# Where the mixer's weight splits are made: three pairs split in the feed-forward, fewer splits on GpSimd, and a rotation that does not wait for its scale

## The chip, the core and the metric

One core of one Trainium2 chip runs the kernel. The metric is device time in microseconds (us), the median of several runs: 1210.14 us before the change (three runs, 1209.3 to 1210.4). The engines are TensorE (PE in the profile, its weight loads PEld), VectorE (DVE), ScalarE (ACT), GpSimd (POOL) and SyncE (SP), which issues the weight loads from HBM.

## The reference

Two layers of an encoder on x of 256 positions by 1024 channels, all in float32:

```python
for l in range(DEPTH):
    x = x + 0.5 * swiglu(rms_norm(x, ffn1_norm[l]), ffn1_w_gate[l], ffn1_w_up[l], ffn1_w_down[l])
    h = rms_norm(x, mix_norm[l])
    u = h @ w_in[l]
    z, xbc, dt_raw, q_lat, kv_lat, k_pe, c_h, c_b, c_c = jnp.split(u, pts, axis=-1)
    ...
    x = x + jnp.concatenate([y_ssd, y_mla, y_conv], axis=-1) @ w_out[l]
    x = x + 0.5 * swiglu(rms_norm(x, ffn2_norm[l]), ffn2_w_gate[l], ffn2_w_up[l], ffn2_w_down[l])
```

The mixer has three branches: a state-space branch (SSD) in both directions over chunks of 128 positions, latent attention (MLA) with 8 heads of 96 channels, 32 of them rotated by position, and a gated convolution. In the attention, q and k are made by two small products from normalised latents, each head's q and k is divided by its root mean square, the last 32 channels are rotated, and softmax attention follows.

## The kernel before, in words

A float32 weight is used as the sum of two numbers that TensorE multiplies in one pass each. For this every weight unit (128 x 1024, or a little less) is loaded into a `raw` tile by SyncE (`issue_dma`, L292), rounded by ScalarE into `whi` (L309), and the rest is subtracted into `wlo` by VectorE or GpSimd (L311, both in `issue_split`). A product is then three matmuls: high by high, high by low, low by high (`mm3`, L435 to L437, or the same three in `project`, `down` and `tokens_mm`). Activations are split likewise after a transposition through PSUM (`split_scaled`, L430 and L432). `whi` and `wlo` have six slots each (`WB`), `raw` three.

The list `specs` holds the loads in the order of use, two units to a load as a rule. `next_unit` hands out the next unit and, before that, issues the splits of the units up to two uses ahead (`AHEAD_SPLIT`). Which splits go to GpSimd stands in `POOL_FFN` (6 of a feed-forward's units, by their place in it) and `POOL_MIX` (24 of a mixer's 55). TensorE's order is the order of the program, written out by hand. The order on the other engines is set by a planner that runs the program on a model of the times; `behind` adds an order where the kernel wants one.

A feed-forward runs over six groups of its 2816 columns (five of 512, one of 256): gate, up, then the down products of the group before. A mixer has a list `main` of units that TensorE works off: after the time-step and latent columns (`tq`) and a first z unit, pairs of 256 columns of `w_in` named in `ORDER`: `('x', i)` are two units of SSD channels (`xbc_unit`), `('c', i)` two of the convolution (`conv_unit`), `('z', i)` one of the gate in two halves, and `('u', 0)` the projection of q, k and v from the latents (`mla_project`). Then come 16 units of `w_out`. `SIDE` says before which place of `main` other work stands on TensorE: the latents' transposes before place 4 (`latents`, L859), the B-C products before 9 (`cb_products`, L870), the transposes of q before 12 and of k before 13 (`mla_transpose`, L957), then per head the scores, the transposes of the probabilities (`mla_turn`, L983) and the products with v, from place 14.

In a channel unit VectorE adds up the convolution's taps (L812) and forms the SiLU (L817). In the convolution branch it does L1032 to L1040, with the transposes at L703. In the attention, `mla_project` copies q and k, sums squares per head (L919), takes the reciprocal root on VectorE (`rsqrt`, L346 to L360), and then calls `mla_rope` for each half of the positions: k is multiplied by its scale (L938, VectorE), and q's and k's last 32 channels are rotated by 12 GpSimd instructions (L943 to L946). In `mla_scores`, VectorE takes the negative maximum of a head's scores for both halves (L972) and multiplies it by q's scale (L974, two numbers per partition); ScalarE's exponential (L977) takes scale and maximum from there. In the SSD heads VectorE does L1113 and L1114.

The buffers `yk` (four of 8 KB a partition) and `b4` (six of 4 KB) belong to the mixer: `yk` holds the transposed q and k and the branches' outputs (and in the first feed-forward the parameter rows), `b4` holds the gate, q and k, and the SSD's tokens and sums.

Of the kernel before, what the change touches and what calls it, by code (L numbers as in the profile page):

```python
# [34 lines left out]
BF16 = mybir.dt.bfloat16  # L35
AHEAD_DMA, AHEAD_SPLIT = 2, 2
WB, NT2, NT1 = 6, 15, 13
# [3 lines left out]

ORDER = [('x', 4), ('c', 0), ('u', 0), ('x', 5), ('x', 1), ('c', 1), ('x', 3), ('x', 0), ('x', 2), ('c', 2), ('c', 3), ('c', 4), ('z', 3), ('c', 5), ('z', 1), ('z', 2)]
SIDE = {'latents': 4, 'cb': 9, 'decays': 6, 'f3': 17, 'qT': 12, 'kT': 13, 'xs0': 18, 'xs1': 22, 'mla': 14, 'mla_b': 1, 'mla_c': 2, 'st': 26, 'mla_out': 23, 'mla_end': 29, 'conv_out': 28, 'conv_end': 30, 'ssd': 18, 'ssd_b': 4, 'end0': 31, 'turn0': 36, 'end1': 40, 'turn1': 42}
POOL_FFN, POOL_MIX = [0, 1, 2, 3, 4, 6], [2, 3, 11, 12, 14, 16, 17, 20, 21, 22, 23, 25, 26, 27, 32, 34, 36, 38, 39, 40, 41, 42, 45, 49]
FREE_FFN, FREE_MIX = [], [4, 5]
# [10 lines left out]
def trunk(ctx: ExitStack, tc: tile.TileContext, I: dict, out: bass.AP):  # L56
# [154 lines left out]

    specs = []

    def cols(w, l, c0, n):
        return w[l, :, c0:c0 + n].rearrange("(k p) f -> p k f", p=P)

    def add(ap, shape, units):
        specs.append((ap, shape, units))

    two = [(slice(None), slice(0, P)), (slice(None), slice(P, 256))]  # L220
# [6 lines left out]

    def spec_ffn(l, n):
        wg, wu, wd = I[f"{n}_w_gate"], I[f"{n}_w_up"], I[f"{n}_w_down"]

        def gu(f0, n):
            for w in (wg, wu):
                if n == 512:
                    for q in range(2):
                        add(w[l, q * 512:(q + 1) * 512, f0:f0 + n].rearrange("(k p) f -> p k f", p=P), (4, n), rr2)
                else:
                    add(cols(w, l, f0, n), (KT, n), kk)

        for i, (f0, n) in enumerate(GROUPS):
            gu(f0, n)  # L240
            if i > 0:
                p0, pn = GROUPS[i - 1]
                for f in range(p0, p0 + pn, 256):
                    rows2(wd[l, f:f + 256, :])
        for f in range(f0, f0 + n, 256):
            rows2(wd[l, f:f + 256, :])

    def spec_mix(l):
# [5 lines left out]
        for kind, i in ORDER:  # L254
            if kind == "x":
                add(cols(w, l, OFF_XBC + i * 256, 256), (KT, 256), two)
            elif kind == "c":
                add(cols(w, l, (OFF_CC, OFF_CH, OFF_CB)[i % 3] + i // 3 * 256, 256), (KT, 256), two)
            elif kind == "z":
                add(cols(w, l, OFF_Z + i * 256, 256), (KT, 256), kk)  # L260
            else:
                add(I["mla_w_uq"][l].rearrange("(k p) f -> p k f", p=P), (2, 768), rr)
                add(I["mla_w_ukv"][l].rearrange("(k p) f -> p k f", p=P), (1, 1024),
                    [(slice(0, 1), slice(None))])
        for c in (6, 7, 4, 5, 0, 1, 2, 3):
            rows2(I["w_out"][l, c * 256:(c + 1) * 256, :])

    pool_units, free_units = set(), set()
    for l in range(DEPTH):
        for n in ("ffn1", "mix", "ffn2"):  # L270
            first = sum(len(s[2]) for s in specs)
            if n == "mix":
# [5 lines left out]
            if first:  # L278
                pool_units.update(first + i for i in (POOL_MIX if n == "mix" else POOL_FFN))
                free_units.update(first + i for i in (FREE_MIX if n == "mix" else FREE_FFN))  # L280

# [17 lines left out]
    def issue_split(i):  # L299
# [6 lines left out]
        _, a, b = src.shape  # L306
        hi = whi.tile([P, 1024], F32R, tag="whi", name=nm("whi"))[:, :a * b].rearrange("p (a b) -> p a b", b=b)
        lo = wlo.tile([P, 1024], F32R, tag="wlo", name=nm("wlo"))[:, :a * b].rearrange("p (a b) -> p a b", b=b)
        i_hi = A.activation(out=hi, in_=src, func=AF.Copy)  # L309
# [20 lines left out]
    def prefetch(n):  # L330
        while st["unit"] <= min(st["use"] + n, len(flat)) - 1:
            issue_split(st["unit"])
            st["unit"] += 1

    def next_unit():
        prefetch(1 + AHEAD_SPLIT)
        i = st["use"]
        st["use"] += 1
        return units.pop(i)

# [378 lines left out]
    def mixer(l, norm, nxt):  # L719
# [168 lines left out]
        def mla_project():  # L888
# [3 lines left out]
            for t in range(NT):  # L892
# [69 lines left out]
        def mla_scores(hh):  # L962
# [191 lines left out]
        for kind, i in ORDER:  # L1154
# [113 lines left out]
```

## Time and profile before

| | us |
|---|---|
| median of 3 runs | 1210.14 |
| lowest, highest | 1209.3, 1210.4 |
| the profiled execution | 1209.31 |
| its span, first to last instruction | 1207.6 |
| TensorE's mean granted clock in it | 0.997 |
| TensorE matmuls busy | 1175.3 |
| VectorE busy | 779.0 |
| ScalarE busy | 656.9 |
| GpSimd busy | 265.7 |

The span is cut into stages here: first feed-forward of layer 0 up to about 200 us, mixer to 415, second feed-forward to 612, then layer 1 with its feed-forward to 797, mixer to 1012 and feed-forward to the end. A table by stretches gives busy time and, in brackets, the number of instructions of each engine, then the granted clock of TensorE, the DMA engines' busy share and the rate. A line of a wait view reads: who waited, for whom, total us, how often, the longest. An instruction that stands still after it has begun counts as busy.

### The profile page before, as it was taken

To read this page: it belongs to the slowest core of one execution; us is meant where nothing else is said; L and a number is where in the kernel's file an instruction comes from. 1 tells how busy PE (TensorE), PEld (TensorE's weight loads), DVE (VectorE), ACT (ScalarE), POOL (GpSimd) and SP (SyncE) were. 2 spreads that over 40 slices of the span, in tenths; PEclk is the share of its full clock that TensorE was granted. 3 is DMA by queue.
4 is the path that set the end of the run, shared out by engine and by line. 5 is a ranking of instruction groups with operands and counts; after the bars stand their busy time and mean duration, and the time that the engine had idled before them with its cause. 6 is when DMAs were issued, how large, how long until landed. Compare 5 with 4: busy or idle time off the path is not lost.

```text
span 1207.6 us, 17054 instructions
## 1 busy us (share of the span) xinstructions
PE 1175.3 (97%) x6540; PEld 1012.8 (84%) x6540; DVE 779.0 (65%) x1283; ACT 656.9 (54%) x1120; POOL 265.7 (22%) x303
## 2 busy tenths in 40 slices
PE   9999999989999999999999999999899999999998
PEld 6888888979978888888888888889799788888887
DVE  6554576898698665554465455469987976555553
ACT  7444456757656564444474444376577556544441
POOL 1140011785252310000040000027832513000000
PEclk9999999999999999999999999999999999999999
DMA  8665554434323465555465555535343334655550
GB/s 281 219 206 176 196 177 132 157 105 133 117 102 140 140 209 180 203 179 201 144 209 188 195 176 196 177 114 165 116 140 106 105 140 151 219 187 175 195 187 35
DMA packets 105537, 198.51 MB, mean 164 GB/s; under 512 B 4014, under 2 KB 47314, under 8 KB 105456
## 3 DMA queue, kind: packets, MB, share of 16 engines
q1 hardware_dynamic: 104288, 197.14, 48.5%
q8 instruction: 51, 0.84, 0.3%
q0 software_dynamic: 1152, 0.28, 0.2%
q14 instruction: 30, 0.25, 0.1%
q10 hardware_dynamic: 16, 0.00, 0.0%
HBM read 196.36 MB, written 1.05 MB: 163 GB/s over the span
## 4 chain that ended last, share of the span: by engine, by line
PE 80%; DVE 11%; ACT 3%; POOL 3%; issue 2%; DMA 0%; SPq 0%; ACTq 0%; DVEq 0%; POOLq 0%
PE ps L577 13%; PE ps L576 13%; PE ps L580 13%; PE ps L528 7%; PE ps L529 7%; PE ps L532 7%; PE ps L437 4%; PE ps L435 4%; PE ps L436 4%; PE ps L599 2%; PE ps L663 1%; DVE wlo L311 1%; PE ps L660 1%; PE ps L661 1%; DVE t L812 1%
## 5 line engine op out<-in xcount | busy, mean ns | idle before, releaser
L309 ACT ACTIVATE whi<-raw 128x1024 fp32r<-128x1024 f32 (+2 forms) x374 | 391.8, 1057 | 394.6 <-PE ps L580 229.7
L311 DVE TENSOR_TENSOR wlo<-raw,whi 128x1024 fp32r<-128x1024 f32 (+1 forms) x308 | 386.5, 1258 | 304.3 <-ACT whi L309 303.6
L576 PE MATMUL ps<-whi,h 128*128 128x512 f32 (+1 forms) x768 | 284.1, 374 | 0.0
L577 PE MATMUL ps<-wlo,h 128*128 128x512 f32 (+1 forms) x768 | 283.4, 373 | 0.1
L311 POOL TENSOR_TENSOR wlo<-raw,whi 128x1024 fp32r<-128x1024 f32 (+2 forms) x66 | 159.4, 2424 | 560.3 <-ACT whi L309 529.0
L580 PE MATMUL ps<-whi,h 128*128 128x512 f32 (+1 forms) x768 | 223.4, 372 | 0.0
L577 PEld LDWEIGHTS ps<-wlo,h 128*128 128x128 f32 x768 | 145.1, 189 | 25.4 <-DVE wlo L311 0.4
L576 PEld LDWEIGHTS ps<-whi,h 128*128 128x128 f32 x768 | 145.0, 189 | 25.1
L580 PEld LDWEIGHTS ps<-whi,h 128*128 128x128 f32 x768 | 140.5, 189 | 25.2
L437 PE MATMUL ps<-h,wlo 128*128 128x256 f32 x384 | 109.4, 285 | 4.5 <-DVE wlo L311 3.1
L435 PE MATMUL ps<-h,whi 128*128 128x256 f32 x384 | 110.8, 288 | 0.1
L436 PE MATMUL ps<-h,whi 128*128 128x256 f32 x384 | 108.8, 283 | 0.0
L528 PE MATMUL ps<-whi,t2r 128*128 128x512 f32 x256 | 101.1, 395 | 0.0
L529 PE MATMUL ps<-wlo,t2r 128*128 128x512 f32 x256 | 99.7, 389 | 0.0
L532 PE MATMUL ps<-whi,t2r 128*128 128x512 f32 x256 | 78.9, 389 | 0.0
L437 PEld LDWEIGHTS ps<-h,wlo 128*128 128x128 f32 x384 | 73.7, 192 | 5.3 <-DVE wlo L311 3.5
L435 PEld LDWEIGHTS ps<-h,whi 128*128 128x128 f32 x384 | 73.9, 192 | 1.2 <-ACT xs L883 0.6
L436 PEld LDWEIGHTS ps<-h,whi 128*128 128x128 f32 x384 | 73.9, 192 | 0.1
L532 PEld LDWEIGHTS ps<-whi,t2r 128*128 128x128 f32 x256 | 48.0, 188 | 10.0
L529 PEld LDWEIGHTS ps<-wlo,t2r 128*128 128x128 f32 x256 | 48.1, 188 | 9.4
L528 PEld LDWEIGHTS ps<-whi,t2r 128*128 128x128 f32 x256 | 48.1, 188 | 9.4
L437 PE MATMUL ps<-whi,t2r 128*128 128x512 f32 (+1 forms) x120 | 46.3, 386 | 2.1 <-DVE t2r L432 2.1
(279 smaller groups left out, 1778.0 us busy)
## 6 DMA issues: line engine op xcount, KB each, us to landing
raw<-in_ffn_w_up SPq DMA_DIRECT2D x44, 1024.0 KB, 5.0
raw<-in_ffn_w_down SPq DMA_DIRECT2D x44, 1024.0 KB, 4.8
raw<-in_ffn_w_gate SPq DMA_DIRECT2D x42, 1024.0 KB, 4.9
raw<-in_w_in SPq DMA_DIRECT2D x32, 1024.0 KB, 4.9
raw<-in_w_out SPq DMA_DIRECT2D x16, 1024.0 KB, 4.9
raw<-in_w_in SPq DMA_DIRECT2D x4, 896.0 KB, 4.6
raw<-in_ffn_w_gate SPq DMA_DIRECT2D x4, 512.0 KB, 6.7
raw<-in_mla_w_uq SPq DMA_DIRECT2D x2, 768.0 KB, 4.1
```

The source lines that it names most:

```text
L309: i_hi = A.activation(out=hi, in_=src, func=AF.Copy)
L311: i_lo = E.tensor_tensor(out=lo, in0=src, in1=hi.bitcast(F32), op=ALU.subtract)
L435: T.matmul(o, sh, mh, start=start, stop=False)
L436: T.matmul(o, sh, ml, start=False, stop=False)
L437: T.matmul(o, sl, mh, start=False, stop=stop)
L528: T.matmul(acc[t][c], yh[:, tsl(t)], wh[:, 0, cs], start=first, stop=False)
L529: T.matmul(acc[t][c], yh[:, tsl(t)], wl[:, 0, cs], start=False, stop=False)
L532: T.matmul(acc[t][c], yl[:, tsl(t)], wh[:, 0, cs], start=False, stop=False)
L576: T.matmul(ps[t], h[:, kt, 0, tsl(t)], w[0][:, i, :], start=kt == 0, stop=False)
L577: T.matmul(ps[t], h[:, kt, 0, tsl(t)], w[1][:, i, :], start=False, stop=False)
L580: T.matmul(ps[t], h[:, kt, 1, tsl(t)], w[0][:, i, :], start=False, stop=kt == KT - 1)
L599: T.transpose(ps[:, j * S + t * P:j * S + (t + 1) * P], a[t][:, f + j * P:f + (j + 1) * P], ident)
```

## The change

- `AHEAD_SPLIT` goes from 2 to 4.
- The pairs x5, x4 and x1 of each mixer are put into the list of loads in groups 3, 4 and 5 of the feed-forward before it (`ffn1`), and their six units are split there into `yk` (x5, x1) and `b4` (x4) tiles instead of slots of `whi` and `wlo`. A list `uses` holds the order of use, which is now another one than that of the loads. None of these six is split by GpSimd.
- `POOL_MIX` keeps 4 of 24 places: 39, 41, 45 and 49, all of `w_out`.
- x5 goes ahead of the projection in `ORDER`, and `mla_project` is put between its two units.
- `mla_rope` is called for each half of the positions as soon as its q and k are copied. It rotates both unscaled; k is multiplied by its scale afterwards, on VectorE as before.
- The product of maximum and scale in `mla_scores` becomes two instructions of one column each.

```diff
-AHEAD_DMA, AHEAD_SPLIT = 2, 2
+AHEAD_DMA, AHEAD_SPLIT = 2, 4
...
-ORDER = [('x', 4), ('c', 0), ('u', 0), ('x', 5), ('x', 1), ...
+ORDER = [('x', 4), ('c', 0), ('x', 5), ('u', 0), ('x', 1), ...
...
-POOL_FFN, POOL_MIX = [0, 1, 2, 3, 4, 6], [2, 3, 11, 12, 14, 16, 17, 20, 21, 22, 23, 25, 26, 27, 32, 34, 36, 38, 39, 40, 41, 42, 45, 49]
+EARLY = [(3, ('x', 5), "yk"), (4, ('x', 4), "b4"), (5, ('x', 1), "yk")]
+POOL_FFN, POOL_MIX = [0, 1, 2, 3, 4, 6], [39, 41, 45, 49]
...
-    def add(ap, shape, units):
+    def add(ap, shape, units, home=None):
+        ids = list(range(n_units[0], n_units[0] + len(units)))
+        n_units[0] += len(units)
         specs.append((ap, shape, units))
+        if home is None:
+            uses.extend(ids)
+        else:
+            homes.update((i, home) for i in ids)
+        return ids
...
+    def pair(l, kind, i, home=None):
+        c0 = OFF_XBC + i * 256 if kind == "x" else (OFF_CC, OFF_CH, OFF_CB)[i % 3] + i // 3 * 256
+        return add(cols(I["w_in"], l, c0, 256), (KT, 256), two, home)
...
+            for g, key, home in EARLY:
+                if n_ == "ffn1" and g == i:
+                    early_units[l, key] = pair(l, *key, home)
...
+            if (l, (kind, i)) in early_units:
+                uses.extend(early_units[l, (kind, i)])
+            elif kind in "xc":
+                pair(l, kind, i)
...
+                uses.append(uses.pop(-4))
...
+    pool_units -= homes.keys()
...
-        hi = whi.tile([P, 1024], F32R, tag="whi", name=nm("whi"))[:, :a * b].rearrange("p (a b) -> p a b", b=b)
-        lo = wlo.tile([P, 1024], F32R, tag="wlo", name=nm("wlo"))[:, :a * b].rearrange("p (a b) -> p a b", b=b)
+        home = homes.get(i)
+        if home == "yk":
+            both = ykp.tile([P, 2, 1024], F32R, tag="yk", name=nm("wyk"))
+            both = both[:, 0, :], both[:, 1, :]
+        elif home == "b4":
+            both = [b4p.tile([P, 1024], F32R, tag="b4", name=nm("wb4")) for _ in range(2)]
+        else:
+            both = (whi.tile([P, 1024], F32R, tag="whi", name=nm("whi")),
+                    wlo.tile([P, 1024], F32R, tag="wlo", name=nm("wlo")))
+        hi, lo = (v[:, :a * b].rearrange("p (a b) -> p a b", b=b) for v in both)
...
-        while st["unit"] <= min(st["use"] + n, len(flat)) - 1:
+        while st["unit"] <= max(uses[st["use"]:st["use"] + n], default=-1):
...
+                mla_rope(t)
             S_["rs"] = small(32)
             V.tensor_scalar(out=S_["rs"], in0=mean_rsqrt(ssq, 32, QK), scalar1=KK, scalar2=None, op0=ALU.mult)
             for t in range(NT):
-                mla_rope(t)
+                rs = S_["rs"][:, t * 16 + 8:t * 16 + 16]
+                V.tensor_tensor(out=qk["k", t], in0=qk["k", t], in1=rs.unsqueeze(2).to_broadcast([P, NH, QK]), op=ALU.mult)
...
-                if key == "k":
-                    rs = S_["rs"][:, t * 16 + 8:t * 16 + 16]
-                    V.tensor_tensor(out=t3, in0=t3, in1=rs.unsqueeze(2).to_broadcast([P, NH, QK]), op=ALU.mult)
...
-            V.tensor_tensor(out=mxn, in0=mx0, in1=rs, op=ALU.mult)
+            for t in range(NT):
+                V.tensor_scalar(out=mxn[:, t:t + 1], in0=mx0[:, t:t + 1], scalar1=rs[:, t:t + 1], scalar2=None, op0=ALU.mult)
...
-                main.append(mla_project)
+                main.insert(-1, mla_project)
```

## Rows read from the trace of the kernel before

**Rows 1.** The page: an engine's busy time, and ScalarE's rounding copies.
```profile
PE 1175.3 (97%) x6540; PEld 1012.8 (84%) x6540; DVE 779.0 (65%) x1283; ACT 656.9 (54%) x1120; POOL 265.7 (22%) x303
...
L309 ACT ACTIVATE whi<-raw 128x1024 fp32r<-128x1024 f32 (+2 forms) x374 | 391.8, 1057 | 394.6 <-PE ps L580 229.7
```

**Rows 2.** Stretches: length, busy PE, PEld, DVE, ACT, POOL; clock, DMA share, GB/s.
```profile
215.00:300.00 85.00, 76.28 (x597) 73.69 (x596) 74.97 (x146) 56.64 (x118) 63.63 (x87) 0.98 0.41 131
300.00:365.00 65.00, 61.74 (x476) 55.10 (x475) 53.20 (x96) 40.81 (x105) 25.54 (x14) 1.00 0.33 112
...
612.00:797.00 185.00, 184.60 (x888) 154.63 (x886) 99.33 (x109) 88.28 (x116) 8.41 (x4) 1.00 0.56 187
812.00:897.00 85.00, 76.76 (x610) 73.60 (x609) 80.05 (x150) 58.12 (x120) 60.87 (x80) 1.00 0.42 136
```

**Rows 3.** TensorE's waits, whole span: for whom, total us, times, longest.
```profile
PE ps L870 <- DVE t L817: 5.3, 2, 2.9
PE ps L437 <- DVE wlo L311: 3.1, 2, 1.5
PE ps L983 <- ACT t L977: 2.7, 2, 2.0
PE ps L703 <- DVE t L1053: 2.7, 2, 1.4
PE ps L437 <- DVE t2r L432: 2.1, 2, 1.1
PE ps L663 <- DVE h L432: 2.0, 2, 1.1
...
PE ps L957 <- DVE qkT L432: 1.5, 1, 1.5
PE ps L437 <- POOL wlo L311: 1.5, 1, 1.5
PE ps L660 <- DVE sz L747: 1.4, 2, 0.7
```

**Rows 4.** Stretches as in 2: the five microseconds with the lower clock.
```profile
285.00:290.00 5.00, 4.18 (x22) 3.94 (x23) 3.83 (x11) 3.50 (x8) 1.67 (x1) 0.66 0.02 5
```

**Rows 5.** Timeline from 282.5: start us, duration us, engine, line, operation, operands.
```profile
282.55 2.34 POOL L311 TENSOR_TENSOR wlo<-raw,whi 128x1024 fp32r<-128x1024 f32 x1
...
282.90 2.01 DVE L974 TENSOR_TENSOR sm<-sm,sm 128x2 f32<-128x2 f32 x1
```

**Rows 6.** Single lines: count, duration in ns min/median/max, first and last start, forms.
```profile
L974 DVE TENSOR_TENSOR sm<-sm,sm x16: 147/615/2014, 277.3 to 913.8; 128x2 f32<-128x2 f32 x16
...
L972 DVE TENSOR_REDUCE sm<-ps x16: 675/682/691, 276.0 to 913.1; 128x2 f32<-128x512 f32 x16
...
L1114 DVE TENSOR_TENSOR t<-t,t x32: 406/422/2615, 305.7 to 977.6; 128x256 f32<-128x256 f32 x32
...
L346 DVE TENSOR_SCALAR sm<-sm x28: 143/154/2406, 15.5 to 1019.6; 128x1 int32<-128x1 int32 x20, 128x16 int32<-128x16 int32 x4, 128x4 int32<-128x4 int32 x2, 128x32 int32<-128x32 int32 x2
...
L358 DVE TENSOR_SCALAR sm<-sm,sm x40: 205/214/216, 18.3 to 1021.1; 128x1 f32<-128x1 f32 x40
```

**Rows 7.** Groups by shape, whole span: count, busy us, mean ns, idle before.
```profile
L1113 DVE TENSOR_TENSOR t<-t 128x256 f32<-128x256 f32 x26 | 20.3, 780 | 15.4 <-ACT t L1111 15.4
L1114 DVE TENSOR_TENSOR t<-t,t 128x256 f32<-128x256 f32 x32 | 19.3, 613 | 0.3
L817 DVE SCALAR_TENSOR_TENSOR t<-t,t 128x256 f32<-128x256 f32 x24 | 15.6, 651 | 1.7 <-ACT t L816 1.7
L974 DVE TENSOR_TENSOR sm<-sm,sm 128x2 f32<-128x2 f32 x16 | 14.9, 933 | 0.2
```

**Rows 8.** Groups by shape in the first mixer (200 to 415), GpSimd, then VectorE.
```profile
L311 POOL TENSOR_TENSOR wlo<-raw,whi 128x1024 fp32r<-128x1024 f32 x23 | 56.5, 2458 | 89.1 <-ACT whi L309 80.6 <-DVE sm L360 8.3 <-DVE k L911 0.2
L943 POOL TENSOR_TENSOR t<-k,tab 128x128 f32<-128x128 f32 x8 | 5.4, 707 | 1.3 <-DVE k L938 1.3
...
L311 DVE TENSOR_TENSOR wlo<-raw,whi 128x1024 fp32r<-128x1024 f32 x27 | 33.1, 1228 | 4.1 <-ACT whi L309 3.9
```

More of the change, by code (lines that the diff above doesn't have):

```diff
@@ L35 @@
 BF16 = mybir.dt.bfloat16
-AHEAD_DMA, AHEAD_SPLIT = 2, 2
+AHEAD_DMA, AHEAD_SPLIT = 2, 4
 WB, NT2, NT1 = 6, 15, 13
 GROUPS = [(f, 512) for f in range(0, 2560, 512)] + [(2560, 256)]
-ORDER = [('x', 4), ('c', 0), ('u', 0), ('x', 5), ('x', 1), ('c', 1), ('x', 3), ('x', 0), ('x', 2), ('c', 2), ('c', 3), ('c', 4), ('z', 3), ('c', 5), ('z', 1), ('z', 2)]
+ORDER = [('x', 4), ('c', 0), ('x', 5), ('u', 0), ('x', 1), ('c', 1), ('x', 3), ('x', 0), ('x', 2), ('c', 2), ('c', 3), ('c', 4), ('z', 3), ('c', 5), ('z', 1), ('z', 2)]
 SIDE = {'latents': 4, 'cb': 9, 'decays': 6, 'f3': 17, 'qT': 12, 'kT': 13, 'xs0': 18, 'xs1': 22, 'mla': 14, 'mla_b': 1, 'mla_c': 2, 'st': 26, 'mla_out': 23, 'mla_end': 29, 'conv_out': 28, 'conv_end': 30, 'ssd': 18, 'ssd_b': 4, 'end0': 31, 'turn0': 36, 'end1': 40, 'turn1': 42}
-POOL_FFN, POOL_MIX = [0, 1, 2, 3, 4, 6], [2, 3, 11, 12, 14, 16, 17, 20, 21, 22, 23, 25, 26, 27, 32, 34, 36, 38, 39, 40, 41, 42, 45, 49]
+EARLY = [(3, ('x', 5), "yk"), (4, ('x', 4), "b4"), (5, ('x', 1), "yk")]
+POOL_FFN, POOL_MIX = [0, 1, 2, 3, 4, 6], [39, 41, 45, 49]
 FREE_FFN, FREE_MIX = [], [4, 5]
@@ L208, in load_params @@
         return turn
-    specs = []
+    specs, uses, homes, early_units = [], [], {}, {}
+    n_units = [0]
     def cols(w, l, c0, n):
         return w[l, :, c0:c0 + n].rearrange("(k p) f -> p k f", p=P)
-    def add(ap, shape, units):
+    def add(ap, shape, units, home=None):
+        ids = list(range(n_units[0], n_units[0] + len(units)))
+        n_units[0] += len(units)
         specs.append((ap, shape, units))
+        if home is None:
[3 more added lines that the diff above has]
+        return ids
     two = [(slice(None), slice(0, P)), (slice(None), slice(P, 256))]
@@ L226, in rows2, with spec_ffn @@
         add(ap.rearrange("(k p) f -> p k f", p=P), (2, D), rr)
-    def spec_ffn(l, n):
-        wg, wu, wd = I[f"{n}_w_gate"], I[f"{n}_w_up"], I[f"{n}_w_down"]
+    def pair(l, kind, i, home=None):
+        c0 = OFF_XBC + i * 256 if kind == "x" else (OFF_CC, OFF_CH, OFF_CB)[i % 3] + i // 3 * 256
+        return add(cols(I["w_in"], l, c0, 256), (KT, 256), two, home)
+    def spec_ffn(l, n_):
+        wg, wu, wd = I[f"{n_}_w_gate"], I[f"{n_}_w_up"], I[f"{n_}_w_down"]
         def gu(f0, n):
@@ L254, in spec_mix @@
         for kind, i in ORDER:
[L255 to L258, printed above, removed]
+            if (l, (kind, i)) in early_units:
+                uses.extend(early_units[l, (kind, i)])
+            elif kind in "xc":
+                pair(l, kind, i)
             elif kind == "z":
@@ L270, in trunk @@
         for n in ("ffn1", "mix", "ffn2"):
-            first = sum(len(s[2]) for s in specs)
+            first = len(uses)
             if n == "mix":
@@ L278, in trunk @@
             if first:
-                pool_units.update(first + i for i in (POOL_MIX if n == "mix" else POOL_FFN))
-                free_units.update(first + i for i in (FREE_MIX if n == "mix" else FREE_FFN))
+                pool_units.update(uses[first + i] for i in (POOL_MIX if n == "mix" else POOL_FFN))
+                free_units.update(uses[first + i] for i in (FREE_MIX if n == "mix" else FREE_FFN))
+    pool_units -= homes.keys()
     raws, units, splits = {}, {}, {}
@@ L338, in next_unit @@
         st["use"] += 1
-        return units.pop(i)
+        return units.pop(uses[i])
     def rsqrt_guess(m, n):
```

## The prediction

> **What bounds the kernel now.** I read the engines' shares first: TensorE's matmuls fill 97% of the span [rows 1], so whatever the change does, it can only win back TensorE's idle time or lose more. Then the busy time by stretch, to find where that idle time lies: the feed-forward stretch has 184.60 us of matmuls in 185 us, nothing to win, while the first mixer has 76.28 in 85 and 61.74 in 65, and the second mixer 76.76 in its 85 [rows 2]. In those stretches VectorE is the fullest engine behind TensorE: 75.0 and 80.1 us of 85 [rows 2]. Then who ends TensorE's waits: nearly all end in VectorE's work, and one in a GpSimd split; the nine rows shown sum to 22.3 us over both mixers [rows 3]. To that comes one clock drop: in the five microseconds from 285 the granted clock is 0.66, so part of them at 1.2 instead of 2.4 GHz, right behind a stretch with several TensorE gaps; 5 x (1 - 0.66) = 1.7 us [rows 4]. So about 24 us of 1209.31 are in play, and the feed-forward cannot get faster.
>
> Why VectorE is late is in two views. A subtraction on GpSimd starts at 282.55 and takes 2.34 us; VectorE's L974, a product of two numbers per partition, starts at 282.90 and takes 2.01 us, until GpSimd is done [rows 5]. By the spread of the lines, L974 takes 0.147 us at best and 2.014 at worst, L1114 0.406 and 2.615, while L972, as close to the splits in time but with one input in PSUM, stays between 0.675 and 0.691 [rows 6]. So VectorE instructions with two SBUF inputs stand still behind a GpSimd split and are booked as busy. So does L346, one input but 32 columns (2.406 us at worst, median 0.154); a one-column scalar product, L358, never does (0.205 to 0.216 in 40) [rows 6].
>
> **The change part by part.**
>
> *GpSimd keeps 4 of 24.* GpSimd has 24 splits in a mixer, 23 of them of 1024 columns at 2.458 us [rows 8]. Twenty leave it; two of these (second unit of x5 and of x1) leave the mixer too, so 18 come to VectorE at 1.23 us (33.1/27, [rows 8]): +22.1 us. The other four units of the three pairs were VectorE's: -4.9 us. What comes back is the blocked time. Over both mixers, with the unblocked lengths of rows 6: L974 14.9 - 16 x 0.147 = 12.5; L1113 26 x (0.780 - 0.406) = 9.7; L1114 32 x (0.613 - 0.406) = 6.6; L817 24 x (0.651 - 0.406) = 5.9 (all three 128x256) [rows 6, 7]; L346 2 x (2.406 - 0.154) = 4.5. That is 39.2 us, 19.6 a mixer. It could be more (small groups are left out) or less (some blocked time stood behind short GpSimd work, which stays); I take it as it is. VectorE then has +22.1 - 4.9 - 19.6 = -2.4 us a mixer, before the next part.
>
> *The maximum times the scale.* L974 becomes two one-column scalar products: 2 x 0.21 = 0.42 us (as L358, [rows 6]) for 0.147 unblocked, +2.2 us a mixer over eight heads. VectorE's work thus ends about where it was, 128 and 133 us of the 150 that 215:365 and 812:962 have (75.0 or 80.1, and 53.20 for the last 65, of which I read the first mixer's row alone [rows 2]), but without single pieces of 2 to 2.6 us in front of what TensorE waits for.
>
> *A rule against the swap.* L358 shows no blocking at one column, L346 does at 32 [rows 6]. The Trainium skill (SBUF — State Buffer, Who interferes with whom) counts `tensor_scalar` among the instructions that can take the port pair shared with GpSimd; if it did so here, each of the new products could stand as long as L974 did, 2.0 us. By the rows the sum is 0.42 a head, by that rule up to 4.0 where a split runs; only four are left, all of output weights, so I keep 0.42.
>
> *Three pairs early.* x5, x4 and x1 are loaded and split in groups 3 to 5 of the first feed-forward, in buffers that stand empty there. Six copies on ScalarE and six subtractions on VectorE move to a stretch where these have 88.28 and 99.33 us of work in 185 [rows 2]: hidden there, nothing on the path. Their three loads of 1 MB (SP's queue, moved past feed-forward loads) bring 187 GB/s at a DMA share of 0.56 [rows 2] by 3 MB in some 90 us, +33 GB/s, to about 220: hidden. If that cover were gone, one late unit costs one TensorE wait, as long as the split waits of now, 1.5 us [rows 3]. In the mixer the six slots of the weight ring no longer hold these six units, so the splits of c1 and x3 can be ready before x5 and x1 are used.
>
> *Four uses ahead.* ScalarE's copies idle mostly until a feed-forward matmul ends (L309 behind L580, 229.7 us in all, [rows 1]), that is, until a slot of the ring of six comes free: they run ahead as far as the ring lets them, so this changes priorities, not room. Between nothing and the two split waits of 3.1 us [rows 3].
>
> *mla_project behind x5's first unit.* The matmuls of the projection now wait for the latents' split (L437 on t2r, 2.1 us in two, [rows 3]). One unit of 24 matmuls in between covers about 85/597 x 24 = 3.4 us [rows 2], more than the 1.1 of one wait: all 2.1 back.
>
> *Rotation from unscaled q and k.* GpSimd's 24 rotation instructions a mixer (0.71 us for a product of k, [rows 8], so at most about 17 us) start when the projection is copied, not when the scale is known. The scaling of k now waits, on VectorE, for GpSimd. Behind it in VectorE's queue stand the evacuations of x1 and c1; if rotation is late, they are too, and so is the ring. That bound is one rotation piece to a few: 0.7 to 3 us a mixer. I take none, since GpSimd has no splits in front of the rotation any more.
>
> **Where each wait goes.** L437 on t2r: 2.1. The B-C products (L870) wait 5.3 for the last x5 channels behind the scale's square root; its L346 alone returns 4.5: 4.5. Late c1 splits on VectorE 3.1: three quarters, 2.3, since they compete with more splits. The GpSimd split: 1.5. Probability transposes (L983) 2.7: L974 returns 2.01 - 0.42 = 1.6, and the clock drop behind it 1.7. kT transposes (L957) 1.5: half, 0.8. The convolution's transposes (L703) 2.7: half, 1.3, as more splits lie on VectorE in 300:365. The z bank (L660) 1.4 and the norm at the mixer's head (L663) 2.0: nothing, no part touches them. Sum 15.8. Against it I set one split's length per mixer as new wait, 2 x 1.23 = 2.5: -13.3 us. From the profiled 1209.31 that is 1196.0; the median of the three runs is 0.83 above the profiled one, so 1196.8.
>
> **The rivals.**
>
> *Slower: VectorE becomes the bound.* If the blocked time does not come back, because the rotation and the logarithms on GpSimd block the same instructions, VectorE has 128.2 + 22.1 - 4.9 + 2.2 = 147.6 us in 150, in the second mixer, from 133.3, 152.7. At the densest stretch seen, 80.05/85 = 94% [rows 2], these take 157 and 162 us: +19, less the 2.1 of the latents: 1227. It turns slower when less than about 9 of the 19.6 us a mixer return (94% of 150 is 141). Against it: the blocks last as long as a split, not as a rotation piece [rows 5, 6]. Chance 9%.
> By the Trainium skill (Perfetto Trace Analysis, Identifying the Most-Contended Engine) occupancy is a fair measure of how near VectorE is to its limit, which would make this rival the forecast. L974's 2.01 us for two columns speaks against it: that busy time is waiting.
>
> *Partial.* Only the waits with a GpSimd split right in front return, with the reordering: 2.1 + 1.5 + 1.6 = 5.2: 1205, and 1203 with the clock drop. TensorE comes earlier to each next point, and VectorE's queue is as full as before. Chance 14%.
>
> *No change.* The order on TensorE is fixed, and the gaps reappear one point later: 1210. For it: VectorE's total work hardly falls. Chance 8%.
>
> *All of it.* Every wait but the norm's: 22.3 - 2.0 + 1.7 = 22.0: 1188. Chance 12%.
>
> **How the numbers follow.** The forecast, 1190 to 1203, has 57%. The range reaches over the partial case and down to the full one: 1187 to 1209. 0.2%, about 2.4 us, is what a measurement here can tell. Faster 0.82 (57 + 14 + 12, less one for the partial case's upper tail), within it 0.08, slower 0.10.
>
> **What would show it.** Right: L974's successor at 0.21 us without tail; L346, L1113, L1114, L817 with maxima near their minima; more L311 on VectorE by 18 a mixer while its busy time in the mixer stands; no wait of L870, L437 on t2r or L983 above 1 us; no second clock drop; rotation over before the scale is known. Wrong: VectorE's busy share above 95% in 215:350 with waits on wlo, waits in the first feed-forward's last groups, or VectorE idle before the k scaling for GpSimd. The forecast fails if the planner puts the added splits in front of the evacuations that TensorE waits for.

## The result and the profile after

The changed kernel takes 1191.24 us (1190.92 to 1191.48) against 1209.72 us for the kernel before on the same chip: ratio 0.9847, interval 0.983 to 0.9864, 18.5 us less. The forecast was 1196.8, range 1187 to 1209. The profiled execution took 1191.48 us, its span is 1189.8 (before 1207.6): 17.8 us less of span. In the changed file the lines lie some 30 further down: the splits L309 and L311 are L340 and L342, the matmuls L435 to L437 are L466 to L468, L663 is L694, L703 is L734, L817 is L848, L870 is L901, L957 is L987, L974 is L1005, L977 is L1008, L983 is L1014, L1114 is L1145.

Where the time went shows when the same matmuls start. Single lines: the 48 matmuls of one line of the output projection (L528, after L559) at the end of each mixer, the first mixer above the second; count, duration in ns min/median/max, first and last start. The kernel before:

```profile
L528 PE MATMUL ps<-whi,yT x48: 389/393/486, 370.8 to 408.1; 128*128 128x512 f32 x48
...
L528 PE MATMUL ps<-whi,yT x48: 389/393/486, 966.8 to 1004.1; 128*128 128x512 f32 x48
```

The same two groups in the changed kernel:

```profile
L559 PE MATMUL ps<-whi,yT x48: 389/393/486, 362.0 to 399.3; 128*128 128x512 f32 x48
...
L559 PE MATMUL ps<-whi,yT x48: 389/393/486, 949.0 to 986.3; 128*128 128x512 f32 x48
```

370.8 to 362.0 is 8.8 us won in the first mixer, 966.8 to 949.0 is 17.8, so 9.0 more in the second. The feed-forwards give nothing and lose nothing: the first matmuls of a channel unit (L437, L468) start at 216.3 and 216.5 us in the first mixer, and at 813.8 and 805.0 in the second, so the second mixer gains on top of an unchanged 8.8.

The page of the changed kernel, engines' busy time, and the shares of the chain that ended last:

```profile
PE 1170.1 (98%) x6540; PEld 1012.7 (85%) x6540; DVE 779.7 (66%) x1339; ACT 656.8 (55%) x1120; POOL 169.8 (14%) x263
...
PE 89%; DVE 5%; ACT 3%; POOL 2%; issue 1%; DMA 1%; SPq 0%; DVEq 0%; ACTq 0%; POOLq 0%
```

Against [rows 1]: VectorE's busy time is the same (779.0 and 779.7), GpSimd's fell by 95.9. TensorE's idle time fell from 32.3 (1207.6 - 1175.3) to 19.7 us, 12.6 less; the other 5.2 us of the 17.8 went out of its busy time (1175.3 to 1170.1) with the same 6540 matmuls. Stretches of the changed kernel: length, busy PE, PEld, DVE, ACT, POOL; clock, DMA share, GB/s.

```profile
215.00:300.00 85.00, 82.24 (x659) 80.74 (x658) 75.65 (x167) 56.62 (x125) 33.21 (x75) 0.98 0.37 120
300.00:365.00 65.00, 62.55 (x481) 56.39 (x480) 54.41 (x111) 43.22 (x110) 12.82 (x9) 1.00 0.30 104
612.00:797.00 185.00, 184.16 (x899) 155.00 (x898) 106.54 (x127) 91.86 (x122) 0.26 (x1) 1.00 0.59 199
812.00:897.00 85.00, 81.12 (x661) 79.08 (x659) 74.97 (x155) 60.63 (x134) 25.43 (x51) 1.00 0.39 125
```

The 85 us from 215 now hold 659 matmuls instead of 597 [rows 2], of another mix, as the work has moved up. The 5.2 us are spread: no group of one line and shape lost more than 0.9 us. My reading, not shown: a matmul's record lasts 0.28 us where the next starts 0.12 us later, so one that is held up by less than the rest leaves no gap in the trace, and the delay stands in "busy".

TensorE's waits over the whole span of the changed kernel, as in [rows 3]:

```profile
PE ps L1014 <- ACT t L1008: 6.6, 6, 2.2
...
PE ps L734 <- DVE t L1084: 2.7, 2, 1.3
PE ps L694 <- DVE h L463: 1.6, 2, 0.8
...
PE ps L466 <- DVE qkT L463: 0.9, 2, 0.5
```

Gone are L870 (5.3), both split waits (3.1 and 1.5), the latents (2.1), L957 (1.5) and L660 (1.4). Not gone are L703 (2.7) and L663 (2.0 to 1.6). The probability transposes, L983's 2.7, grew to 6.6, and the clock still drops behind them, in the five microseconds from 275 instead of those from 285 [rows 4]; stretches of five microseconds in the changed kernel:

```profile
270.00:275.00 5.00, 2.70 (x21) 2.26 (x20) 4.93 (x15) 3.12 (x8) 0.00 (x0) 0.97 0.26 73
275.00:280.00 5.00, 5.00 (x33) 5.00 (x32) 4.93 (x11) 3.30 (x8) 0.00 (x0) 0.69 0.40 142
```

Why, is in the timelines of VectorE and ScalarE from 270 (start, duration, line, operands):

```profile
270.19 0.68 DVE L1002 TENSOR_REDUCE sm<-ps 128x2 f32<-128x512 f32 x1
...
271.18 1.22 DVE L342 TENSOR_TENSOR wlo<-raw,whi 128x1024 fp32r<-128x1024 f32 x1
...
272.45 0.33 DVE L1005 TENSOR_SCALAR sm<-sm,sm 128x1 f32<-128x1 f32 x2
...
272.13 1.04 ACT L340 ACTIVATE whi<-raw 128x1024 fp32r<-128x1024 f32 x1
273.08 0.55 ACT L1008 ACTIVATE t<-ps,sm,sm 128x256 f32<-128x256 f32 x1
```

The product no longer stands 2.01 us [rows 5]. Between the maximum and the product VectorE now does a split, so the product starts 1.6 us after the maximum ended (270.87 to 272.45). But that is not what the exponential (L1008) waits for last: the product is done at 272.8, and the exponential starts at 273.08, when ScalarE's own rounding copy (L340), which stands ahead of it in ScalarE's order, is done. So it is wherever TensorE waits for L1008. At the first head of each mixer (2.19 us) the head's first exponential starts 0.3 us after the product, at the sixth (waits of 0.73 and 0.37) 1.05 us after it, each time right behind a copy; the copy at the sixth head had itself waited 2.8 us for a matmul (L467). In the kernel before, ScalarE stood idle for 3.35 us at the wait of 285 and began its exponential 0.1 us after L974: there the product did end the wait.

What became of the instructions that stood still behind GpSimd, groups by shape (count, busy us, mean ns):

```profile
L1145 DVE TENSOR_TENSOR t<-t,t 128x256 f32<-128x256 f32 x32 | 20.2, 633 | 0.1
L1144 DVE TENSOR_TENSOR t<-t 128x256 f32<-128x256 f32 x26 | 14.1, 541 | 9.4 <-ACT t L1142 7.5 <-PE ps L913 1.8
L848 DVE SCALAR_TENSOR_TENSOR t<-t,t 128x256 f32<-128x256 f32 x24 | 10.7, 448 | 0.0
L1005 DVE TENSOR_SCALAR sm<-sm,sm 128x1 f32<-128x1 f32 x32 | 5.3, 206 | 0.1
```

Against [rows 7], L1113 gave back 6.2 of its 9.7 blocked us, L817 4.9 of 5.9, L974 all 12.5; L1114 nothing (19.3 and 20.2). What is left blocked stands behind GpSimd work that stays: the longest L1145 (2.50 us) and L1144 (2.00 us) lie beside two of the splits that GpSimd keeps, others of 0.9 to 1.3 us beside its L1125 of the SSD.

### The profile page after: what moved, and what is told of

It reads as the page before. It is cut to its first block, busy times and chain, and to the rows that moved or that the text cites. A ratio compares the mean times of both kernels' runs of the same rounds, so it can differ in the third digit from the quotient of the medians.

```text
span 1189.8 us, 17034 instructions
## 1 busy us (share of the span) xinstructions
PE 1170.1 (98%) x6540; PEld 1012.7 (85%) x6540; DVE 779.7 (66%) x1339; ACT 656.8 (55%) x1120; POOL 169.8 (14%) x263
## 3 DMA queue, kind: packets, MB, share of 16 engines
HBM read 196.36 MB, written 1.05 MB: 166 GB/s over the span
## 4 chain that ended last, share of the span: by engine, by line
PE 89%; DVE 5%; ACT 3%; POOL 2%; issue 1%; DMA 1%; SPq 0%; DVEq 0%; ACTq 0%; POOLq 0%
PE ps L607 14%; PE ps L608 14%; PE ps L611 13%; PE ps L559 7%; PE ps L560 7%; PE ps L563 7%; PE ps L466 5%; PE ps L468 5%; PE ps L467 5%; PE ps L694 2%; PE ps L691 2%; PE ps L630 2%; PE ps L692 2%; DVE wlo L342 1%; PE ps L1154 1%; PE ps L1023 1%
## 5 line engine op out<-in xcount | busy, mean ns | idle before, releaser
L342 DVE TENSOR_TENSOR wlo<-raw,whi 128x1024 fp32r<-128x1024 f32 (+2 forms) x336 | 416.8, 1245 | 288.5 <-ACT whi L340 287.3
L340 ACT ACTIVATE whi<-raw 128x1024 fp32r<-128x1024 f32 (+1 forms) x362 | 379.7, 1057 | 388.0 <-PE ps L611 211.2
L342 POOL TENSOR_TENSOR wlo<-raw,whi 128x1024 fp32r<-128x1024 f32 x26 | 63.4, 2448 | 411.9 <-ACT whi L340 395.0
L559 PE MATMUL ps<-whi,t2r 128*128 128x512 f32 x256 | 101.0, 395 | 0.0
L466 PE MATMUL ps<-h,whi 128*128 128x256 f32 x288 | 83.7, 291 | 0.0
L467 PE MATMUL ps<-h,whi 128*128 128x256 f32 x288 | 81.9, 284 | 0.0
L468 PE MATMUL ps<-h,wlo 128*128 128x256 f32 x288 | 81.8, 284 | 0.0
L466 PEld LDWEIGHTS ps<-h,whi 128*128 128x128 f32 x288 | 55.6, 193 | 1.0 <-DVE t L1063 0.5
L559 PEld LDWEIGHTS ps<-whi,t2r 128*128 128x128 f32 x256 | 48.1, 188 | 9.4
L467 PEld LDWEIGHTS ps<-h,whi 128*128 128x128 f32 x288 | 55.7, 193 | 0.0
L468 PEld LDWEIGHTS ps<-h,wlo 128*128 128x128 f32 x288 | 55.6, 193 | 0.0
L843 DVE SCALAR_TENSOR_TENSOR t<-ps,pt,t 128x254 f32<-128x254 f32 (+1 forms) x96 | 45.9, 478 | 5.4 <-ACT t L839 4.1
```

The lines of the kernel that those rows point to most:

```text
L342: i_lo = E.tensor_tensor(out=lo, in0=src, in1=hi.bitcast(F32), op=ALU.subtract)
L466: T.matmul(o, sh, mh, start=start, stop=False)
L467: T.matmul(o, sh, ml, start=False, stop=False)
L468: T.matmul(o, sl, mh, start=False, stop=stop)
L559: T.matmul(acc[t][c], yh[:, tsl(t)], wh[:, 0, cs], start=first, stop=False)
L843: st["gate_dve"] = V.scalar_tensor_tensor(out=ac[:, o0:o1], in0=ps[:, o0 + sh:o1 + sh], scalar=col("cw", k * 12 + ct), in1=ac[:, o0:o1], o ...
```

## The experiments

The theory: VectorE's two-input instructions stood behind GpSimd's splits, and once they do not, TensorE's waits on VectorE go; the rest of the change is worth little. The rivals: the rest of the change (order, pairs, depth, rotation) makes the gain, or the gain needs several parts at once. The kernel before, run beside each, took 1209.0 to 1209.7 us, so times can be compared across the runs. One thing goes through all of them: the planner lays out VectorE, ScalarE and GpSimd anew for each kernel, so the cost of a part undone holds what the new order on these engines costs or saves, and that share was not separated.

**The splits back on GpSimd.** All else as changed; 22 splits of a mixer on GpSimd again (the two places that are now early pairs fall away).

```diff
-POOL_FFN, POOL_MIX = [0, 1, 2, 3, 4, 6], [39, 41, 45, 49]
+POOL_FFN, POOL_MIX = [0, 1, 2, 3, 4, 6], [2, 3, 12, 13, 17, 20, 21, 22, 23, 25, 26, 27,
+    32, 34, 36, 38, 39, 40, 41, 42, 45, 49]
```

> The changed kernel with GpSimd's places given back: 22 of the 24 (its list in the new order of use; the two units that are now split in the feed-forward stay off GpSimd). If VectorE's two-input instructions standing behind GpSimd splits were the main cause of the gaps (theory A), L1005's successor in the score chain is clear of it, but the other VectorE lines get maxima of 2 us and more again, and the time rises by 8 to 13 us, to 1199 to 1204. If the early pairs and the new order on TensorE made the gain (theory B), it stays within 1191 to 1194.

Measured 1208.46 us, ratio 0.9997 (0.9987 to 1.0007): without this part the others give nothing. TensorE's waits in it:

```profile
PE ps L987 <- DVE qkT L463: 8.5, 4, 3.9
PE ps L1014 <- ACT t L1008: 5.9, 12, 1.3
```

and the product with the scale, beside 62 splits on GpSimd (single line):

```profile
L1005 DVE TENSOR_SCALAR sm<-sm,sm x32: 196/204/216, 277.0 to 913.5; 128x1 f32<-128x1 f32 x32
```

28 of these 32 lie wholly inside a split on GpSimd, so the one-column product is never held up, splits or not. The Trainium skill (SBUF — State Buffer, Who interferes with whom) lists `tensor_scalar` among the instructions that can enter a mode that takes the shared port pair, when their operands meet the mode's conditions; in this form it was not seen to.

**The splits alone, in the kernel before.** The reverse: only POOL_MIX changes.

```diff
-POOL_FFN, POOL_MIX = ..., [2, 3, 11, 12, 14, 16, 17, 20, 21, 22, 23, 25, 26, 27, 32, 34, 36, 38, 39, 40, 41, 42, 45, 49]
+POOL_FFN, POOL_MIX = ..., [39, 41, 45, 49]
```

> The kernel before with GpSimd's mixer places cut from 24 to the four of output weights and nothing else: 20 more splits a mixer on VectorE. Theory A: about 25 us a mixer of blocked VectorE time goes, 24.6 us of splits come; the pieces of 2 us in front of TensorE's waits are gone, so 1199 to 1204. If VectorE becomes the bound, as it has 20 splits more and none fewer: 1211 to 1225. Theory B: 1208 to 1212.

Measured 1203.96 us, ratio 0.996 (0.9946 to 0.9974): 5.0 us less than the kernel before. The blocked time has gone already; groups by shape of this kernel:

```profile
L1114 DVE TENSOR_TENSOR t<-t,t 128x256 f32<-128x256 f32 x32 | 20.1, 632 | 0.2
L1113 DVE TENSOR_TENSOR t<-t 128x256 f32<-128x256 f32 x26 | 13.9, 535 | 11.4 <-ACT t L1111 10.5 <-PE ps L882 0.9
L817 DVE SCALAR_TENSOR_TENSOR t<-t,t 128x256 f32<-128x256 f32 x24 | 10.9, 456 | 0.0
L974 DVE TENSOR_TENSOR sm<-sm,sm 128x2 f32<-128x2 f32 x16 | 2.4, 152 | 0.1
```

These are the lengths of the changed kernel; L974 takes 0.152 instead of 0.933 us with its two SBUF inputs unchanged. That GpSimd's splits were what blocked it is thus shown. The same section of the Trainium skill (SBUF — State Buffer, Who interferes with whom) has a VectorE instruction with two SBUF inputs contend with a GpSimd instruction that reads SBUF; these runs agree. But TensorE now waits elsewhere:

```profile
PE ps L957 <- POOL q L946: 6.5, 2, 3.9
PE ps L983 <- ACT t L977: 4.5, 4, 1.7
PE ps L437 <- DVE t2r L432: 2.9, 2, 1.5
```

The rotation on GpSimd, which hid behind other waits, is late by 3.9 us.

**The rotation undone.** In the changed kernel, k is scaled first and rotated behind the root again.

```diff
-                mla_rope(t)
             S_["rs"] = small(32)
...
                 V.tensor_tensor(out=qk["k", t], in0=qk["k", t], in1=rs.unsqueeze(2)...
+                mla_rope(t)
```

> The changed kernel with the rotation put back behind the scale (k multiplied first, both halves rotated after the reciprocal root). With GpSimd's places cut alone, TensorE's kT and qT transposes waited 6.5 us for the rotation. If the unscaled rotation is what takes that wait away, it returns here: 1196 to 1199. If the early pairs or the new order had taken it away already, 1191 to 1193.

Measured 1207.11 us, ratio 0.9982 (0.9973 to 0.9992): 15.9 us more than the changed kernel, nearly all of the gain. Its waits, and GpSimd's last rotation step in the first mixer (timeline):

```profile
PE ps L987 <- POOL q L976: 12.8, 2, 6.4
...
263.90 0.46 POOL L976 TENSOR_TENSOR k<-t 128x128 f32<-128x128 f32 x1
```

and the same step in the changed kernel:

```profile
248.18 0.46 POOL L976 TENSOR_TENSOR k<-t 128x128 f32<-128x128 f32 x1
```

The rotation ends 15.7 us later when it starts behind the scale. Six microseconds of that reach TensorE in each mixer; on top the clock falls four times in the two mixers instead of once.

**Splits and rotation in the kernel before.** If these two were the gain, they would give it together.

```diff
-POOL_FFN, POOL_MIX = ..., [2, 3, 11, ...
+POOL_FFN, POOL_MIX = ..., [39, 41, 45, 49]
...
+                mla_rope(t)
...
-                mla_rope(t)
...
+                V.tensor_tensor(out=qk["k", t], in0=qk["k", t], in1=rs.unsqueeze(2)...
...
-                if key == "k":
...
```

> The kernel before with two parts of the change: GpSimd's places cut to four, and the rotation from unscaled q and k. Cut alone gave 1204 and left waits of 6.5 us for the rotation. If the parts are steps of one chain, the pair gives more than the two singly: 1196 to 1199. If the missing early pairs and depth hold VectorE back all the same, 1202 to 1205.

Measured 1204.25 us (1200.75 to 1205.13), ratio 0.9948 (0.993 to 0.9966). No more than the splits alone. The wait on GpSimd has gone and late splits have come, 5.0 us instead of the 0.8 that they took with the splits alone (L982 and L976 are L983 and L977 in this file):

```profile
PE ps L437 <- DVE wlo L311: 5.0, 6, 1.5
PE ps L982 <- ACT t L976: 4.3, 3, 1.7
```

**The depth of the splits undone.**

```diff
-AHEAD_DMA, AHEAD_SPLIT = 2, 4
+AHEAD_DMA, AHEAD_SPLIT = 2, 2
```

> The changed kernel with splits issued two uses ahead in place of four. If the ring of six slots sets how far splits run ahead, 1190 to 1193; if the depth does, waits on wlo come back in the mixers and the time is 1193 to 1198.

Measured 1201.69 us, ratio 0.9933 (0.9918 to 0.9948): 10.5 us. Waits, and VectorE's timeline around one of them:

```profile
PE ps L468 <- DVE wlo L342: 4.1, 4, 1.9
PE ps L467 <- DVE wlo L342: 3.2, 2, 1.6
...
234.81 1.22 DVE L342 TENSOR_TENSOR wlo<-raw,whi 128x1024 fp32r<-128x1024 f32 x1
...
238.02 1.01 DVE L950 TENSOR_REDUCE sm<-t 128x4 f32<-128x384 f32 x2 [1.40 <-ACT t L948]
```

The same place in the changed kernel:

```profile
234.09 2.62 DVE L342 TENSOR_TENSOR wlo<-raw,whi 128x1024 fp32r<-128x1024 f32 x2
```

With depth four two splits are done in one go, behind two rounding copies on ScalarE (from 231.93 us on). With depth two one copy and one split are done, and VectorE then stands idle for 1.40 us in front of a reduction that waits for ScalarE. The next copy starts on ScalarE at 245.26 us and the next split on VectorE at 249.37. So the depth does not only change priorities: both halves of the next split stand behind other work in the order of their engines, and idle time ahead of that is of no use to them. This is one place; that it makes all of the 10.5 us is not shown.

**The early pairs undone.**

```diff
-EARLY = [(3, ('x', 5), "yk"), (4, ('x', 4), "b4"), (5, ('x', 1), "yk")]
+EARLY = []
```

> The changed kernel with no pair split in the feed-forward: x5, x4 and x1 in the ring again, all on VectorE. Six splits, 7.3 us of VectorE and 6.4 of ScalarE, come back to each mixer. If VectorE's work in the first 100 us of the mixer sets the pace, 1194 to 1201. If the ring of six was ahead enough, 1191 to 1193.

Measured 1197.03 us, ratio 0.9901 (0.9884 to 0.9917): 5.8 us. Between 200 and 365 VectorE has 36 splits instead of 31, about 6 us more work, and L1014's wait grows from 6.6 to 7.5, with 1.4 new where a unit's first matmul (L466) waits for the convolution's product L1063, and 0.8 at L901.

**The projection's place undone.**

```diff
-ORDER = [('x', 4), ('c', 0), ('x', 5), ('u', 0), ('x', 1), ...
+ORDER = [('x', 4), ('c', 0), ('u', 0), ('x', 5), ('x', 1), ...
...
-                main.insert(-1, mla_project)
+                main.append(mla_project)
```

> The changed kernel with the projection ahead of both units of x5 again. The recorded sum: the two waits for the latents' split return, 2.1 us and the half microsecond of the high part, so 1193 to 1195. If VectorE is now early enough with that split for lack of blocking, 1191 to 1192.

Measured 1194.2 us (1191.19 to 1196.53), ratio 0.9873 (0.9851 to 0.9894). The ratio's interval overlaps that of the changed kernel, so the size stays open; the latents' wait is back, 1.1 us in two.

**One product for both halves.**

```diff
-            for t in range(NT):
-                V.tensor_scalar(out=mxn[:, t:t + 1], in0=mx0[:, t:t + 1], scalar1=rs[:, t:t + 1], ...
+            V.tensor_tensor(out=mxn, in0=mx0, in1=rs, op=ALU.mult)
```

> The changed kernel with maximum times scale as one product of two SBUF inputs again (0.15 us unblocked for 0.42 in two pieces). No GpSimd split is left near the scores, so if only those block it, 1190 to 1192. If the short GpSimd work left there (logarithm, SSD sums) blocks it, or the probabilities' wait (6.6 us in the changed kernel) is set by this pair, 1193 to 1196 in the first case and 1188 to 1190 in the second.

Measured 1192.16 us, ratio 0.9858 (0.9844 to 0.9873), not to be told from the changed kernel. The product takes 0.152 us (0.148 to 0.165 in 16). Once the splits have gone, nothing blocks it, and the swap is worth nothing that shows. Nor could it at the first heads, where ScalarE's copy ends after the product.

**GpSimd kept busy without moving work.** The changed kernel with a GpSimd subtraction of two constant tiles, read by nobody, at 18 of the places a mixer that GpSimd had before; for room NT2 is 13 instead of 15. The second kernel has the marks and NT2 = 13 but no subtraction.

```diff
-WB, NT2, NT1 = 6, 15, 13
+WB, NT2, NT1 = 6, 13, 13
...
+        if i in shadow_units:
+            mark = G.tensor_copy(out=small(1), in_=hi.bitcast(F32)[:, 0, 0:1])
+            wide = [m.unsqueeze(1).to_broadcast([P, 8, P]) for m in (ident, LI)]
+            behind(G.tensor_tensor(out=shade, in0=wide[0], in1=wide[1], op=ALU.subtract), mark)
```

> The changed kernel, and at 18 places of each mixer GpSimd also subtracts two constant 1024-column views into a tile that nobody reads, behind a one-column copy that waits for the unit's whi; every result of the kernel is as before. Two buffers of the t2 pool (15 to 13) make room. If VectorE stands still while GpSimd reads two SBUF inputs (theory A), the time is 10 to 25 us above that of the same kernel without the large subtraction, and VectorE's lines show maxima over 2 us. If GpSimd's splits hurt because their result came late (theory C), nothing waits for these, and the time is within 1 us of it.

> The same without the large subtraction: the one-column copies and the two missing t2 buffers alone. All theories: 1191 to 1195, as it only serves to be compared with.

Measured 1249.43 us with it (ratio 1.0338, 1.0317 to 1.0359), 1205.15 without (0.9967, 0.9955 to 0.9978). Engines' busy time with it, and its subtraction:

```profile
PE 1190.9 (95%) x6540; PEld 1030.5 (82%) x6540; DVE 830.6 (66%) x1339; ACT 658.3 (53%) x1120; POOL 275.5 (22%) x335
...
L349 POOL TENSOR_TENSOR shade<-ident,LI x36: 2341/2394/3227, 196.3 to 997.2; 128x1024 f32<-128x1024 f32 x36
```

and without:

```profile
PE 1173.9 (98%) x6540; PEld 1016.0 (85%) x6540; DVE 781.6 (65%) x1339; ACT 657.0 (55%) x1120; POOL 188.8 (16%) x299
```

VectorE does the same 1339 instructions and is booked 49.0 us longer; the kernel takes 44.3 us longer, 1.2 us for each of 36 subtractions whose result nobody reads. This is the price of GpSimd beside a full VectorE, and it comes in two parts. TensorE's waits grow, and behind them its clock falls more often: the mean granted clock of the profiled executions is 0.973 with the subtraction and 0.992 without. Priced by (1 - clock) x span, as if TensorE had no idle time, that is 33.8 against 9.6 us, an estimate of up to 24 of the 49.5 us between these two executions. That the kernel without the subtraction is 14 us over the changed one was not expected. Its largest wait is 8.7 us, in two, of the transposes at a mixer's head for the norm's scaled rows; whether the two buffers fewer or the marks make it was not separated. The price of the subtraction is the difference of the two kernels, in which both stand alike.

**Two tries at the waits that are left.** The attention's turn and values one unit later (for L1014), and the convolution's output one unit earlier (for L734).

```diff
-SIDE = {... 'mla_b': 1, 'mla_c': 2, ... 'mla_out': 23, ...
+SIDE = {... 'mla_b': 2, 'mla_c': 3, ... 'mla_out': 24, ...
```

> The changed kernel with each head's probability transposes, the products with v behind them and the attention's end one unit later (two units after the scores in place of one). The transposes wait 6.6 us for exponentials that come late from VectorE's queue, and a clock drop of 1.7 us follows in the first mixer. If one unit of 24 matmuls, about 2.9 us, is the missing cover, 1184 to 1187. If VectorE's queue is the bound in that stretch, the wait moves to the next point and it is 1190 to 1193.

Measured 1191.36 us, ratio 0.9853 (0.9838 to 0.9867): no change. (That the exponentials come late from VectorE's queue was my reading then; ScalarE's rows above show its copies ahead of them.) L1014's wait and the clock drop behind it have gone, but TensorE now waits for L848:

```profile
PE ps L913 <- DVE t L848: 4.5, 2, 2.3
```

```diff
-SIDE = {... 'conv_out': 28, ...
+SIDE = {... 'conv_out': 27, ...
```

> The changed kernel with one step of the convolution's branch moved: the transposes, squares and norm of its output (L1073 to L1085) are placed one unit of matmuls earlier (27 instead of 28), so that three units instead of two lie between them and the transposes back (L1088, L734), which wait for the VectorE product L1084 twice, 2.7 us in all, in the changed kernel. Theory A (every one of TensorE's remaining waits ends in VectorE's queue, and a wait is the place where the hand-written order gives that queue too little lead): the wait at L734 goes below 0.5 us and the time is 1187.5 to 1189.5, unless VectorE's queue is full there, and in 345 to 365 us it isn't. Theory B (VectorE's queue is the bound here too, as it was when the attention's turns came one unit later): L734's wait goes, a wait of about the same size comes at a neighbouring point, in front of the unit that now lies behind the moved step or at the transposes L1077, and the time stays at 1190.5 to 1192.5.

Measured 1195.12 us, ratio 0.9877 (0.986 to 0.9893): 3.9 us worse, which neither theory had. L734's 2.7 us went, a wait of 3.6 us came one point earlier, and the clock drops twice more, at 862 and 934:

```profile
PE ps L1109 <- DVE o L1123: 3.6, 2, 2.4
...
860.00:865.00 5.00, 3.42 (x17) 3.19 (x18) 4.93 (x14) 4.26 (x9) 0.00 (x0) 0.73 0.66 213
865.00:870.00 5.00, 5.00 (x43) 5.00 (x42) 3.37 (x8) 2.35 (x7) 0.00 (x0) 0.93 0.16 34
930.00:935.00 5.00, 2.56 (x6) 1.01 (x5) 4.69 (x15) 0.07 (x1) 1.07 (x2) 0.90 0.31 125
935.00:940.00 5.00, 5.00 (x30) 3.87 (x30) 2.93 (x6) 3.18 (x8) 1.75 (x2) 0.76 0.01 3
```

The waits account for 0.9 us of the 3.9 (3.6 - 2.7). The two drops, priced as in the prediction, are 5 x (0.27 + 0.07) and 5 x (0.10 + 0.24) = 1.7 us each, 3.4 together: 4.3 where 3.9 are to be explained, the drops being priced as if TensorE had no idle time in them.

## Why the prediction was right, and where it was not

The sign, the place (both mixers, nothing in the feed-forwards) and the reason hold: the splits blocked VectorE, and giving them to VectorE cost it nothing net. The sum came out 5.2 us short (13.3 against 18.5), by errors of both signs. That the time still lies in the forecast's 1190 to 1203 is in part luck: at L983 and its clock drop the sum was 7.2 us too high, and 5.2 us came out of TensorE's busy time, which it had at nothing.

- *GpSimd keeps 4: right in the sum, not in its terms.* VectorE's splits go from 386.5 to 431.0 us in all, and its busy time rises by 0.7, so the blocked time came back. But L1114's 6.6 us did not (20.1 us with the splits alone, 20.2 after): I put down to the splits that move what hangs on GpSimd work that stays, the four kept splits and the SSD's L1125. Of the 39.2 us counted, 26.6 returned (12.5 + 6.2 + 4.9 + 3.9 of L346 - 0.9). The rest came from small groups that I had left out, L360, 12.3 us before and 8.8 after (L391), and L1034, 8.6 and 3.6 (L1065), among them.
- *The maximum times the scale: right on its length, wrong on the wait.* It takes 0.206 us and has no tail. The step that failed is "L974 returns 1.6": it took the product for the last thing on the path from the maximum to the transposes. In the changed kernel ScalarE's rounding copies stand ahead of the exponentials and end last, L1014's wait is 6.6 instead of 1.1, and the clock drop stayed (1.7). I had named added splits in front of what TensorE waits for as what would break the forecast, but thought of VectorE's half of a split alone, and priced it at 2.5 us for both mixers in no place. Why the copies come to stand there (the depth, the pairs or the planner) is not shown.
- *Three pairs early: hidden in the feed-forward, as said, but worth more.* No wait came there; undone, they cost 5.8 us. I gave them no gain beyond the ring's slots. They also take 5 splits out of VectorE's fullest stretch.
- *Four uses ahead: the term that was most mis-sized.* "Priorities, not room", 0 to 3.1 us; undone, it costs 10.5. By [rows 1] ScalarE's copies wait for slots in the kernel as a whole, and that is a reading of the feed-forward. In the mixer the place of the copy and the split in their engines' order counts as well, as the idle 1.40 us show.
- *mla_project behind x5: as said.* The latents' wait went (2.1) and came back in part (1.1) when undone; the time it is worth is not clear of the noise.
- *Rotation: no wait, as taken, but no gain counted either.* It ended at 248.6, before the scale at 251.7. Left as it was, it costs 15.9 us, because TensorE comes to the transposes earlier than before: q's start at 263.8 us in the kernel before and at 257.6 in the changed one, while the rotation's last step ends at 264.5 in the kernel before and at 264.4 with the rotation undone. The step that failed is the list of waits: it held those of the kernel before alone, and one that was hidden behind them (the rotation) was not on it.
- *Where each wait goes.* L870, both split waits, t2r: 10.4 by the sum, 12.0 measured. L957: 0.8 and 1.5. L660 and L663: 0 and 1.8. L703: 1.3 and 0; the two units between the convolution's norm and its transposes are too short: the wait is 2.7 us in most of the kernels here, and goes with a third unit between. L983 and the clock: 3.3 and -3.9 (2.7 to 6.6, the drop as before). New waits: 2.5 and 0.9. By the rows shown that is 10.5 us won where the sum had 13.3; TensorE's idle time fell by 12.6. Of the other 2.1, four small waits that are no longer listed give 2.5 (L1078 1.2, L1104 0.7, L435 0.4, L992 0.2), the wait for x at the very start took 1.0 more (1.8 to 2.8), and 0.6 is in none of the waits listed. And 5.2 us came out of TensorE's busy time, which no row of [rows 3] could hold.
- *The rivals.* Slower (VectorE the bound): with the blocks gone it did not come; the kernel with GpSimd kept busy shows that it would have with the blocks still there, at 1249, of which 14 us come without the subtraction too. Partial, 1205: this is what the splits alone give (1203.96), and the splits with the rotation. No change: what the other parts without the splits give (1208.46). All of it, 1188: nearer to the result than the forecast.

The Trainium skill (Perfetto Trace Analysis, Identifying the Most-Contended Engine) takes occupancy as a fair measure for VectorE and not for matmuls. This case agrees on the second (TensorE's busy time fell by 5.2 us with the same 6540 matmuls) and not on the first: VectorE's occupancy is the same 66% in the changed kernel and in the one with 36 subtractions that nobody reads, 58 us apart.

Undone one at a time, the parts cost 17.2, 15.9, 10.5, 5.8 and 3 us, together 52 of a gain of 18.5; for the first three I had expected 8 to 13, 5 to 8 and 2 to 7. The splits alone give 5.0. So the theory's first half holds, and its second, that the rest is worth little, does not. My reading: each part removes one of several waits in a row on the same chain; with one of the large ones back, TensorE waits there, and much of what the others won is lost at that place. What stays open: how much of the last 13 us (1204.25 to 1191.24) is the pairs and how much the depth, for the two were not tried one without the other on top of splits and rotation in the kernel before; and what bounds the changed kernel in 215 to 300, where moving L1014's wait brought another of 4.5 us. VectorE, with 75.65 of 85 us busy there, is the likely one, argued and not shown; the order on ScalarE, which ended L1014's waits, has its part in it.

## What to carry to other kernels

Look at the spread of an instruction's length before moving work between GpSimd and VectorE: where the longest is as long as a GpSimd operation beside it, VectorE's busy time is partly waiting, and work taken over from GpSimd can cost nothing. Cost a change of several parts along the chain of all that TensorE would wait for, the hidden ones too, since the first part alone gives little when a second wait stands right behind. Where a split stands in the order of its engine counts as much as how long it is: ask what the engine does in its idle time, and what stands, on every engine of the path, between a result and the one who waits for it.

## What the runs showed of the hardware

The same gap lowers TensorE's clock or does not. In the changed kernel TensorE waits 2.19 us for L1008 in the second mixer, and the clock stays at 1.00; timeline, and the stretch around it:

```profile
862.38 0.87 PE L1014 MATMUL ps<-ident,t 128*128 128x128 f32 x3 [2.19 <-ACT t L1008]
...
860.00:865.00 5.00, 2.71 (x22) 2.27 (x20) 4.93 (x12) 4.47 (x11) 0.00 (x0) 1.00 0.58 182
```

In the kernel with the convolution's output one unit earlier, the same wait, behind the same kind of matmuls, is 2.18 us, and the granted clock of the stretch, shown above, is 0.73:

```profile
861.47 0.99 PE L1014 MATMUL ps<-ident,t 128*128 128x128 f32 x4 [2.18 <-ACT t L1008]
```

The first mixer's gap of the same length did lower it, to 0.69, in the changed kernel, and with one product for both halves the gap of 2.19 us lowers it in both mixers (0.66 and 0.72). What decides is not shown. So a drop of about 1.7 us can come or stay away behind the same wait, and differences of that size between two kernels need their clock rows before a reason is given.
